# The last 256 output columns, one token tile at a time, with the layer norm of the first tile between the two

## The chip, the cores and the metric

The kernel runs on one core of a Trainium2 chip. The metric is the time of one execution in device microseconds; of a kernel that was run several times the median counts. The kernel before took 1534.78 us (median of three runs, 1531.65 to 1538.52).

The engines are named as in the profile: PE is TensorE (PEld its weight load), DVE is VectorE, ACT is ScalarE, POOL is GpSimd, and SP is the engine from whose queue nearly all transfers are issued here.

## What is computed

Two transformer-like blocks follow each other on 256 tokens of 2048 features, all in float32. The part that the change touches is the end of the second block: the last product (the output of the forgetting attention times `w_out`), the gated residual, and the layer norm that gives the result.

```python
def layer_norm(x, g, b):
    mu = jnp.mean(x, axis=-1, keepdims=True)
    var = jnp.mean(jnp.square(x - mu), axis=-1, keepdims=True)
    return (x - mu) * lax.rsqrt(var + EPS) * g + b

# last layer of the second block; y has 2048 features for each of the 256 tokens
out = y @ w_out
x = layer_norm(DN_ALPHA * x + gate[:, None] * out, ln_g[1], ln_b[1])
```

The mean and the variance of a token run over all 2048 columns, so nothing of a token's result can be written before its last column has been multiplied.

## The kernel before

**Tiling.** The 256 tokens are two token tiles of 128 (`ti` 0 and 1). Weights come in chunks of 128 x 1024 float32 (512 KB) from DRAM into one of seven `raw` buffers. ACT rounds a chunk to its high part `hi` (L1603), DVE forms the rest `lo` (L1605), and PE multiplies three times, high by high, high by low and low by high. `hi` and `lo` have three buffers each, and a chunk is prepared two chunks ahead of its use.

**The last product** (`o3` in the code). The first 1024 columns are one range of 16 chunks. The other 1024 columns are four ranges of 256 columns, each of four chunks, a chunk holding four row tiles of 256 columns. In `mm_tok` the activations are stationary and the weights stream: for each row tile, both token tiles get three products of 256 columns, so 24 products a chunk and 96 a range. Both token tiles of a range lie in one PSUM bank.

**After each range.** `evac_out(i)` runs on DVE: for the two token tiles the product times the gate (L1423), plus the residual (L1425), and the statistics of the finished columns (L1427, `bn_stats`). It is written in pairs: L1423 for both tiles, L1425 for both, L1427 for both. All 2048 columns of both tiles end up in `xk`, the first 1024 already times the gain.

**The bias rows.** After the third of the four ranges `evac_out` starts `bias_rows`, which puts the bias of the first 1024 columns under a product of one row of ones: four PE products of 1 x 128 by 1 x 512, two at the next step of the scheduler and two one chunk later. They fill four PSUM banks `vb`.

**The end.** `finish` runs after the last range, for both token tiles together. On DVE: the moments (L1452), the reciprocal root by `rsqrt` (L170 to L182, three rounds of two dependent steps, for one column a tile), with four operations of 512 columns (L1457, `center`) placed between the steps, and the row `wfo` = -mean times the root (L1461). Meanwhile `warm(20)` gives PE 20 products that nobody reads. Then PE turns `wfo` (L1466), ACT copies it (L1467), four one-row products add `wfo` times the gain into the `vb` banks, and DVE forms the eight pieces of 512 columns of the result (L1475), each followed by its store of 256 KB from the SP queue (L1476).

**What sets the order.** The program is written in one sequence by Python code: one loop over the chunks prepares, multiplies and calls the range's `evac`, and a small scheduler (`sched.tick`) advances side tasks once a chunk. Each engine runs its instructions in that order, and semaphores join the engines. Buffers of 128 x 1024 for the attention and the end come from one pool `blk` of 15.

Of the kernel before, what the change touches and what calls it, by code (L numbers as in the profile page):

```python
# [9 lines left out]
F32 = mybir.dt.float32  # L10
# [6 lines left out]
P = 128  # L17
# [15 lines left out]
W1 = 5  # L33
# [8 lines left out]
WARM = 20  # L42
# [30 lines left out]
class Slice:  # L73
    """Columns of a modulation product, summed over the 16 row tiles, per of them to a chunk; TensorE takes tiles pe."""
# [7 lines left out]
class Chunk:  # L82
    """Row tiles kts of a weight, 1024 / len(kts) columns of each."""
# [6 lines left out]
class Range:  # L90
    """Output columns of a product, 512 token columns to a bank; kind says which operand is stationary."""
# [7 lines left out]
def two_block_kernel(ctx: ExitStack, tc: tile.TileContext, a: dict, out: bass.AP):  # L99
# [47 lines left out]
    def warm(n):  # L147
        """Keeps TensorE's clock up while it waits: products that nothing reads."""
# [16 lines left out]
    def rsqrt(y, v, between=()):  # L165
        """rsqrt of two columns, in as few dependent steps as there can be; other work between the steps."""
        between = list(between)
        t, vh = t_([P, 2], "rq2"), t_([P, 2], "rqh")
# [4 lines left out]
        c = [slice(i, i + 1) for i in range(2)]  # L173
# [85 lines left out]
    def start(kind):  # L259
        """A head starts some ticks after the one before it."""  # L260
# [107 lines left out]
    def broadcast_cols(cols, dst):  # L368
        """cols: [128 tokens, n x 1]; dst [128, n*128] has each column along its free axis."""
# [12 lines left out]
    def dilated_tables():  # L382
        """-|t - s|, hugely negative where no dilation reaches s from t, and the number of dilations that do."""
# [28 lines left out]
    def retention_tables():  # L412
        """t - s where t >= s, s - t where s >= t, else huge, as [s, t]; the log decays."""
# [22 lines left out]
    def causal_tables():  # L436
        """s - t, hugely negative where s > t, blocks [(t1,s0) (t1,s1) (t0,s0)]; the mask of a diagonal block."""
# [17 lines left out]
    def logsig(dst, x, e, u, w):  # L455
        """min(x, 0) - log1p(exp(-|x|)), log1p(e) = 2 atanh(e / (2 + e))."""
# [59 lines left out]
    def colsum(sl):  # L516
        """Sums over partitions of the slice's columns, as columns [128, columns / 128]."""
# [22 lines left out]
    def shift_scale(sl, i, A, B, bshift, bscale, gain, beta, key):  # L540
        """A = gain * (1 + scale), B = shift + beta * (1 + scale) for the slice's column tiles from i on."""
# [41 lines left out]
    def mod_ss(w, ccol, A, B, bshift, bscale, gain, beta, key, i, n_=4):  # L583
        """Shift and scale of the features of n_ tiles from i on."""
# [37 lines left out]
    def affine_split(key, t, A, B, kt, fast=False):  # L622
        """First half of the split of A * t + B; returns the second half."""
# [62 lines left out]
    def begin_h(g):  # L686
        """Starts the activations that chunks up to g + HLEAD need; returns their second halves."""
# [11 lines left out]
    def mm_feat(r, ck, hi, lo):  # L699
        """Weights stationary: result [features, tokens]."""  # L700
# [9 lines left out]
    def mm_tok(r, ck, hi, lo):  # L710
        """Activations stationary: result [tokens, features]."""
# [27 lines left out]
    def add_range(w, c0, kts, kind, act, evac, per=1):  # L739
        """Columns c0.. of w over the row tiles kts, per row tiles to a chunk."""  # L740
# [7 lines left out]
    def add_segs(w, ranges, segs, act, evac):  # L748
        """segs: (indices of ranges, first row tile, last + 1), in order."""
# [5 lines left out]
    def gate_task(name):  # L755
        """z becomes 2 silu(z), in place."""
# [13 lines left out]
    # block 1 projections, in groups of row tiles  # L770
# [208 lines left out]
    def ret_gate(h):  # L979
# [4 lines left out]
        done("qkr", 2, 4)  # L984
        done("zr", 2, 4)

# [1 line left out]
    sums = {}  # L988

    def residual(r, k0, g):  # L990
# [702 lines left out]
```

## Time and profile before

| what | value |
|---|---|
| median of three runs | 1534.78 us (1531.65 to 1538.52) |
| profiled execution, span from the first to the last instruction | 1533.4 us |
| mean granted TensorE clock | 0.991 |
| PE busy | 1491.9 us, 97% of the span |
| DVE busy | 1264.8 us, 82% |
| ACT busy | 821.8 us, 54% |
| HBM read and written | 433.88 and 2.11 MB |
| last range of 256 columns, first to last product begun | 1499.55 to 1516.13 us |
| from the start of the last of them to the end of the last DVE operation | 1516.13 to 1530.20 us |

The span is the only time of that execution that the profile states, and it is the one against which the prediction's sum is made. Of its 1533.4 us, 3.2 us come after the last DVE operation: the last store and the end of the program. A line such as L145 is the line of the code that issued an instruction; L145 is the helper for every product. A product of float32 by float32 shows as two PE records, one of rounded parts as one.

### The profile page before, as it was taken

How to read it: one execution, taken by the hardware profiler on the slowest of the kernel's cores; microseconds unless marked ns; L12 is line 12 of the kernel's file. 1: busy time of each engine (PE TensorE's matmuls, PEld its weight loads, DVE VectorE, ACT ScalarE, POOL GpSimd, SP SyncE). 2: the span in 40 equal slices, each digit the busy share in tenths (PEclk: the TensorE clock that was granted, in tenths of full speed). 3: DMA queues.
4: the chain of work that ended last, by engine and by line, in shares of the span. 5: the costliest groups of instructions: out<-in, count | busy, mean ns of one | idle time of the engine just before them, and what ended most of it. 6: DMA issues, size and time to landing. Idle time of an engine off the chain costs nothing.

```text
span 1533.4 us, 26873 instructions
## 1 busy us (share of the span) xinstructions
PE 1491.9 (97%) x10190; PEld 1385.7 (90%) x10190; DVE 1264.8 (82%) x1832; ACT 821.8 (54%) x1532; POOL 49.6 (3%) x50
## 2 busy tenths in 40 slices
PE   5899999999999999999999999999999999999998
PEld 5889999989999798899998899978899999999897
DVE  5889989999988887987879988988887956667784
ACT  4474463655644657444555653465444776667530
POOL 3500000021000000000000000000000000000000
PEclk9999999999999999999999999999999999999998
DMA  9899979879699798999888889867899966878741
GB/s 321 289 353 338 344 273 324 309 255 328 213 322 326 250 366 282 343 343 311 254 297 286 295 301 320 272 210 250 320 354 324 338 231 199 260 259 292 259 152 56
DMA packets 180358, 437.77 MB, mean 285 GB/s; under 512 B 16352, under 2 KB 51314, under 8 KB 180228
## 3 DMA queue, kind: packets, MB, share of 16 engines
q1 hardware_dynamic: 179620, 435.89, 82.6%
q8 instruction: 80, 1.31, 0.3%
q14 instruction: 50, 0.41, 0.1%
q0 software_dynamic: 544, 0.14, 0.1%
q10 hardware_dynamic: 64, 0.02, 0.0%
HBM read 433.88 MB, written 2.11 MB: 284 GB/s over the span
## 4 chain that ended last, share of the span: by engine, by line
PE 81%; DVE 10%; ACT 3%; DMA 3%; issue 2%; SPq 0%; DVEq 0%; ACTq 0%
PE pa L145 74%; PE ps L145 4%; DVE lo L1605 4%; DVE acc L1588 3%; DMA w<-fdr 1%; ACT hi L1603 1%; PE ps L527 1%; DMA raw<-in_w_ada_dram 1%; DMA raw<-in_x_dram 1%; DVE hy L635 0%; DMA raw<-in_a_w_in_dram 0%; ACT w L632 0%; PE ps L1171 0%; DVE xT L656 0%; ACT blk L788 0%
## 5 line engine op out<-in xcount | busy, mean ns | idle before, releaser
L145 PE MATMUL pa<-hy,hi 128*128 128x256 f32 x4640 | 854.0, 286 | 8.7 <-ACT hy L631 2.7
L1603 ACT CAST hi<-raw 128x1024 fp32r<-128x1024 f32 x464 | 485.5, 1048 | 530.1 <-PE pa L145 444.2
L145 PEld LDWEIGHTS pa<-hy,hi 128*128 128x128 f32 x4640 | 726.3, 192 | 14.1 <-ACT hy L631 3.1
L1605 DVE TENSOR_TENSOR lo<-raw,hi 128x1024 fp32r<-128x1024 f32 x464 | 568.9, 1228 | 204.5 <-ACT hi L1603 200.8
L145 PE MATMUL pa<-hy,lo 128*128 128x256 f32 x2320 | 658.9, 284 | 1.9 <-DVE lo L1605 1.9
L145 PE MATMUL pa<-hi,hy 128*128 128x512 f32 (+1 forms) x1536 | 463.7, 380 | 3.2 <-ACT hy L631 2.3
L145 PEld LDWEIGHTS pa<-hy,lo 128*128 128x128 f32 x2320 | 445.5, 192 | 2.9 <-DVE lo L1605 2.5
L1588 DVE SCALAR_TENSOR_TENSOR acc<-raw,cact,acc 128x1024 f32<-128x1024 f32 (+2 forms) x343 | 423.0, 1236 | 8.8 <-DMA raw<-in_w_ada_dram 8.0
L145 PEld LDWEIGHTS pa<-hi,hy 128*128 128x128 f32 x1536 | 284.4, 192 | 58.7 <-ACT hy L631 3.4
L145 PE MATMUL pa<-lo,hy 128*128 128x512 f32 (+1 forms) x768 | 288.5, 376 | 1.1 <-DVE lo L1605 1.1
L145 PEld LDWEIGHTS pa<-lo,hy 128*128 128x128 f32 x768 | 147.2, 192 | 26.1 <-DVE lo L1605 1.7
L788 ACT ACTIVATE blk<-pa 128x512 f32<-128x512 f32 (+1 forms) x96 | 51.7, 578 | 10.9 <-PE pa L145 8.3
L535 ACT ACTIVATE jk<-ps 128x128 f32<-128x128 f32 x158 | 43.6, 276 | 9.9 <-PE ps L527 6.1
L792 DVE TENSOR_TENSOR blk<-pa,blk 128x512 f32<-128x512 f32 x60 | 37.4, 681 | 0.3 <-PE pa L145 0.3
L145 PE MATMUL ps<-blk,blk 128*128 128x256 f32 (+1 forms) x176 | 37.3, 342 | 0.0
L145 PEld LDWEIGHTS ps<-blk,blk 128*128 128x128 f32 x176 | 30.1, 190 | 3.3 <-DVE blk L792 0.2
L635 DVE TENSOR_TENSOR hy<-w,hy 128x256 fp32r<-128x256 f32 x64 | 27.1, 425 | 5.9 <-ACT w L632 4.9
L535 ACT ACTIVATION_READ_ACCUMULATOR jk<-ps 128x1 f32 x158 | 30.7, 195 | 0.0
L1573 POOL MEMSET acc<- 128x1024 f32 x2 | 1.9, 950 | 859.7 <-PE ps L527 859.7
L632 ACT ACTIVATE w<-xT,B,A 128x256 f32<-128x256 f32 x32 | 19.2, 600 | 11.3 <-DVE xT L662 11.3
L527 PE MATMUL ps<-ident,acc 128*128 128x128 f32 x160 | 24.6, 278 | 0.0
L634 ACT CAST hy<-w 128x256 fp32r<-128x256 f32 x58 | 23.6, 407 | 1.9
(295 smaller groups left out, 821.1 us busy)
## 6 DMA issues: line engine op xcount, KB each, us to landing
raw<-in_w_mod_dram SPq DMA_DIRECT2D x192, 512.0 KB, 5.3
raw<-in_a_w_in_dram SPq DMA_DIRECT2D x128, 512.0 KB, 5.6
raw<-in_w_in_dram SPq DMA_DIRECT2D x112, 512.0 KB, 5.4
raw<-in_w_ada_dram SPq DMA_DIRECT2D x80, 512.0 KB, 5.4
raw<-in_kv_w_mod_dram SPq DMA_DIRECT2D x64, 512.0 KB, 6.0
raw<-in_kv_w_dram SPq DMA_DIRECT2D x64, 512.0 KB, 5.3
raw<-in_b_w_in_dram SPq DMA_DIRECT2D x64, 512.0 KB, 5.0
raw<-in_w_out_dram SPq DMA_DIRECT2D x32, 512.0 KB, 5.3
```

The costliest lines, as they stand in the source:

```text
L145: PE.matmul(o, l, r, start=start, stop=stop, skip_group_check=True)
L527: PE.transpose(pt[:, j * P : (j + 1) * P], sl.acc[:, (q + j) * P : (q + j + 1) * P], ident)
L535: AC.activation(jk, pt[:, j * P : (j + 1) * P], AF.Copy, accum_out=r[:, q + j : q + j + 1])
L632: AC.activation(hf, t, AF.Identity, bias=bi, scale=sc)
L634: AC.copy(h[:, 0, :], hf)
L635: V.tensor_tensor(h[:, 1, :], hf, h[:, 0, :].bitcast(F32), op=ALU.subtract)
L788: AC.activation(dst, src, AF.Copy, scale=sc)
L792: V.tensor_tensor(dst, src, dst, op=ALU.add)
L1573: GP.memset(sl.acc, 0.0)
L1588: V.scalar_tensor_tensor(ac, tn, c, ac, op0=ALU.mult, op1=ALU.add)
L1603: AC.copy(hi, t)
L1605: V.tensor_tensor(lo, t, hi.bitcast(F32), op=ALU.subtract)
```

## The change

The first three ranges of 256 columns stay, but `evac_out` now finishes one token tile (`add_part`: times the gate, plus the residual, statistics) before it turns to the other.

The last range has a kind of its own, `last`, and two PSUM banks, one for each token tile. Its chunks are multiplied for tile 0 as they come, and kept; the `hi` and `lo` of its fourth chunk take two `blk` buffers, since the three `hi` and `lo` buffers hold the first three chunks. Then tile 0 goes through its statistics, its root and its first two stores, while PE multiplies the same four chunks for tile 1. After three of these four chunks PE turns tile 0's row, and after the fourth it makes tile 0's products. `finish` then treats tile 1 alone, with tile 0's other two pieces and stores in between.

The bias rows are gone. `wfo` has a second column of ones, and the gain and the bias lie in two rows of one buffer, so that one product of two rows gives the shift and the bias together: four such products instead of four for the bias and four for the shift. Twenty unread products become five. The bias of the last 1024 columns is loaded earlier in the SP queue. Docstrings and comments are removed.

```diff
-WARM = 20
+WARM = 5
...
-        for nm in "gb":
-            yield need_blk(1)
-            lnr[nm + "r", 0] = blk()
-            nc.sync.dma_start(lnr[nm + "r", 0][0:1, :], a[f"ln_{nm}_2"][1:2, 0:CW])
+        yield need_blk(1)
+        lnr["gb"] = blk()
+        for i, nm in enumerate("gb"):
+            nc.sync.dma_start(lnr["gb"][i : i + 1, :], a[f"ln_{nm}_2"][1:2, 0:CW])
         yield need_blk(1)
         lnr["b"] = blk()
         nc.sync.dma_start(lnr["b"], a["ln_b_2"][1, CW:D].partition_broadcast(P))
...
+    def add_part(i, ti, src):
+        x = out_part(ti, CW + i * S, S)
+        t = t_([P, S], "w1", W1)
+        V.tensor_tensor(t, src, gbc[1][:, i * S : (i + 1) * S], op=ALU.mult)
+        V.tensor_tensor(x, x, t, op=ALU.add)
+        V.bn_stats(bst[:, ti, 2 + i, :], x)
...
-            for ti in (1, 0):
-                V.tensor_tensor(t[ti], r.banks[0][:, ti * S : (ti + 1) * S], gbc[1][:, i * S : (i + 1) * S], op=ALU.mult)
-            for ti in range(2):
-                V.tensor_tensor(x[ti], x[ti], t[ti], op=ALU.add)
-            for ti in range(2):
-                V.bn_stats(bst[:, ti, 2 + i, :], x[ti])
-            if i == 2:
-                sched.add(bias_rows(), front=True)
-            if i == 3:
-                finish()
+            for ti in (1, 0):
+                add_part(i, ti, r.banks[0][:, ti * S : (ti + 1) * S])
...
+    def shifts(wr):
+        u = []
+        for c in range(2):
+            u.append(pacc.tile([P, 512], F32, tag="acc", name=uid("pa")))
+            mm(u[c], wr[0:2, 0:P], lnr["gb"][0:2, c * 512 : (c + 1) * 512], True, True)
+        return u
...
+    def mm_last(r, ck, hi, lo):
+        r.kept.append((ck, hi, lo))
+        one_tile(r, 0, [r.kept[-1]])
+        if not ck.last:
+            return
...
+        add_part(3, 0, r.banks[0][:, 0:S])
+        moments(0, [lambda c=c: center(0, c) for c in (2, 3)])
+        for c in (2, 3):
+            store(0, c, lnb(c))
+        one_tile(r, 1, r.kept[:3])
+        wr = shift_row(0)
+        one_tile(r, 1, r.kept[3:])
+        r.u0 = shifts(wr)
...
+    def finish(r):
+        add_part(3, 1, r.banks[1][:, 0:S])
+        moments(1, [lambda: center(1, 2), lambda: store(0, 0, r.u0[0]), lambda: center(1, 3),
+                    lambda: store(0, 1, r.u0[1])])
         warm(WARM)
+        u = shifts(shift_row(1))
         for c in (2, 3, 0, 1):
+            store(1, c, u[c] if c < 2 else lnb(c))
...
+            if ck.kind == "last" and ck.last:
...
+                hi, lo = (blkp.tile([P, CW], F32R, tag="blk", name=uid("blk")) for _ in range(2))
```

Three places in the order of the instructions follow. The first is DVE between the third and the fourth range, before. `w` is the product times the gate, `blk_15291` and `blk_15380` are tiles 0 and 1 of the last 1024 columns, and the last two rows prepare the third and fourth chunk of the last range.

```order
L1423 TENSOR_TENSOR w_16598<-pa_16488,blk_16209 128x256
L1423 TENSOR_TENSOR w_16597<-pa_16488,blk_16209 128x256
L1425 TENSOR_TENSOR blk_15291<-blk_15291,w_16597 128x256
L1425 TENSOR_TENSOR blk_15380<-blk_15380,w_16598 128x256
L1427 BN_STATS bst<-blk_15291 128x6
L1427 BN_STATS bst<-blk_15380 128x6
L1605 TENSOR_TENSOR lo_16610<-raw_16392,hi_16609 128x1024
L1605 TENSOR_TENSOR lo_16643<-raw_16422,hi_16642 128x1024
```

The same place after the change, where `blk_15299` and `blk_15388` are tiles 0 and 1:

```order
L1419 TENSOR_TENSOR w_16604<-pa_16495,blk_16216 128x256
L1420 TENSOR_TENSOR blk_15388<-blk_15388,w_16604 128x256
L1421 BN_STATS bst<-blk_15388 128x6
L1419 TENSOR_TENSOR w_16608<-pa_16495,blk_16216 128x256
L1420 TENSOR_TENSOR blk_15299<-blk_15299,w_16608 128x256
L1421 BN_STATS bst<-blk_15299 128x6
L1645 TENSOR_TENSOR lo_16613<-raw_16399,hi_16612 128x1024
L1645 TENSOR_TENSOR blk_16631<-raw_16429,blk_16630 128x1024
```

The pairs have become two chains of three dependent operations, and the two `lo` operations still stand behind them.

The second place is PE from the end of the third range into the fourth, before; `ps_16605` and `ps_16607` are banks of the bias, `pa_16613` is the bank of the last range.

```order
L145 MATMUL pa_16488<-lo_16514,hy_15986 128x256
L145 MATMUL pa_16488<-hi_16513,hy_15986 128x256
L145 MATMUL ps_16605<-blk_15825,ones 128x512
L145 MATMUL ps_16607<-blk_15825,ones 128x512
L145 MATMUL pa_16613<-hi_16541,hy_15259 128x256
L145 MATMUL pa_16613<-lo_16542,hy_15259 128x256
```

After the change nothing stands between the ranges; the row of tile 0 is turned inside the products of tile 1 (`pa_16617`), between its third and its fourth chunk (`blk_16630` and `blk_16631` are that chunk's high and low part):

```order
L145 MATMUL pa_16617<-hi_16612,hy_15933 128x256
L145 MATMUL pa_16617<-lo_16613,hy_15933 128x256
L145 MATMUL pa_16617<-hi_16612,hy_15933 128x256
L1451 MATMUL ps_16732<-ident,wfo_125 2x128
L145 MATMUL pa_16617<-blk_16630,hy_15935 128x256
L145 MATMUL pa_16617<-blk_16631,hy_15935 128x256
```

The four bias products have left PE's queue, and one turning product that waits for DVE now stands ahead of tile 1's last twelve products.

The third place is the end of PE's queue, before; `xT` with `ident` are the unread products.

```order
L145 MATMUL pa_16755<-xT,ident 128x256 x20
L1466 MATMUL ps_16776<-ident,wfo 1x128 x2
L145 MATMUL ps_16605<-blk_15823,s_16777 128x512
L145 MATMUL pa_16638<-blk_15823,s_16777 128x512
L145 MATMUL ps_16607<-blk_15823,s_16777 128x512
L145 MATMUL pa_16640<-blk_15823,s_16777 128x512
```

And after:

```order
L145 MATMUL pa_16748<-blk_15831,s_16734 128x512
L145 MATMUL pa_16750<-blk_15831,s_16734 128x512
L145 MATMUL pa_16776<-xT,ident 128x256 x5
L1451 MATMUL ps_16782<-ident,wfo_126 2x128
L145 MATMUL pa_16786<-blk_15831,s_16784 128x512
L145 MATMUL pa_16788<-blk_15831,s_16784 128x512
```

Tile 0's two products have moved ahead of the unread ones, and two instead of four follow the last turning.

## Rows read from the trace of the kernel before

**Rows 1.** The chain that ended last, from 1440 us: start, length, engine and line.

```profile
1497.71 1.91 PE ps L145 x4
```

**Rows 2.** Stretches: length; busy us of PE, PEld, DVE, ACT, POOL; granted clock; DMA.

```profile
1461.00:1497.43 36.43, 36.43 (x294) 35.39 (x293) 28.92 (x41) 13.54 (x14) 0.00 (x0) 1.00 0.42 134
1497.43:1499.55 2.12, 2.12 (x7) 0.74 (x5) 1.77 (x5) 1.04 (x1) 0.00 (x0) 1.00 0.04 8
1499.55:1503.90 4.35, 4.35 (x24) 4.35 (x24) 1.54 (x3) 0.00 (x0) 0.00 (x0) 0.61 0.00 0
1503.90:1506.02 2.12, 2.12 (x8) 0.74 (x6) 0.73 (x1) 1.04 (x1) 0.00 (x0) 1.00 0.00 0
1506.02:1516.25 10.23, 10.23 (x74) 10.23 (x74) 0.50 (x1) 0.00 (x0) 0.00 (x0) 0.83 0.00 0
```

**Rows 3.** PE in order of time, around the end of the third range: start, length, operation.

```profile
1496.59 0.28 PE L145 MATMUL pa<-lo,hy 128*128 128x256 f32 x1
...
1496.95 0.28 PE L145 MATMUL pa<-lo,hy 128*128 128x256 f32 x1
...
1500.94 0.41 PE L145 MATMUL pa<-lo,hy 128*128 128x256 f32 x1
...
1501.58 0.41 PE L145 MATMUL pa<-lo,hy 128*128 128x256 f32 x1
```

**Rows 4.** PE in order of time, from the last product of the last range.

```profile
1516.13 0.28 PE L145 MATMUL pa<-hi,hy 128*128 128x256 f32 x1
1516.25 8.79 PE L145 MATMUL pa<-xT,ident 128*128 128x256 f32 x40
1524.88 0.38 PE L1466 MATMUL ps<-ident,wfo 128*1 128x128 f32 x2
1525.71 1.12 PE L145 MATMUL ps<-blk,s 1*128 1x512 f32 x2 [0.45 <-ACT s L1467]
```

**Rows 5.** DVE in order of time, third range's end and after the last product.

```profile
1499.88 1.21 DVE L1605 TENSOR_TENSOR lo<-raw,hi 128x1024 fp32r<-128x1024 f32 x1
...
1516.45 0.75 DVE L1423 TENSOR_TENSOR w<-pa,blk 128x256 f32<-128x256 f32 x2 [9.93 <-PE pa L145]
1517.23 0.76 DVE L1425 TENSOR_TENSOR blk<-blk,w 128x256 f32<-128x256 f32 x2
...
1518.58 0.47 DVE L1452 BATCH_NORM_AGGREGATE mvo<-bst 128x2 f32<-128x36 f32 x2
1519.08 0.17 DVE L1453 TENSOR_SCALAR vfo<-mvo 128x2 f32<-128x2 f32 x1
...
1519.57 0.74 DVE L1457 SCALAR_TENSOR_TENSOR blk<-blk,mvo,blk 128x512 f32<-128x512 f32 x1
1520.23 0.34 DVE L178 SCALAR_TENSOR_TENSOR rq<-yfo,rqh 128x1 f32<-128x1 f32 x2
...
1523.64 0.16 DVE L1461 SCALAR_TENSOR_TENSOR wfo<-mvo,yfo 128x2 f32<-128x2 f32 x1
...
1526.87 0.75 DVE L1475 SCALAR_TENSOR_TENSOR blk<-blk,yfo,ps 128x512 f32<-128x512 f32 x1 [0.42 <-PE ps L145]
...
1529.45 0.75 DVE L1475 SCALAR_TENSOR_TENSOR blk<-blk,yfo,pa 128x512 f32<-128x512 f32 x1
```

**Rows 6.** DVE operations after 1516.3 us by line: count, busy us, mean ns, idle.

```profile
L178 DVE SCALAR_TENSOR_TENSOR rq<-yfo,rqh 128x1 f32<-128x1 f32 x6 | 1.0, 214 | 0.0
L1423 DVE TENSOR_TENSOR w<-pa,blk 128x256 f32<-128x256 f32 x2 | 0.8, 420 | 9.9 <-PE pa L145 9.9
```

**Rows 7.** Two earlier stretches in which PE stood idle; columns as in rows 2.

```profile
1355.40:1361.20 5.80, 3.38 (x27) 3.33 (x28) 1.58 (x2) 5.66 (x11) 0.00 (x0) 1.00 0.74 268
999.50:1007.80 8.30, 4.61 (x12) 2.88 (x13) 5.45 (x27) 4.72 (x10) 0.00 (x0) 0.83 0.15 58
```

**Rows 8.** The SP queue in order of time: start, length, line, transfer.

```profile
1414.77 0.23 SPq L1378 DMA_DIRECT2D blk<-in_ln_b_dram  x1
1419.04 2.65 SPq L1552 DMA_DIRECT2D raw<-in_b_w_out_dram  x2
...
1430.57 0.37 SPq L1381 DMA_DIRECT2D blk<-in_ln_b_dram  x1
```

More of the change, by code (lines that the diff above doesn't have):

```diff
@@ L172, in rsqrt @@
         V.tensor_scalar(yi, yi, -1, 0x5F3759DF, op0=ALU.mult, op1=ALU.add)
-        c = [slice(i, i + 1) for i in range(2)]
+        c = [slice(i, i + 1) for i in range(n_)]
         for _ in range(3):
@@ L1384, in two_block_kernel @@
     bst = c_([P, 2, 6, 6], "bst")
-    vb = {}
     def out_part(ti, c0, n_):
@@ new lines, in f, with center @@
+                add_part(i, ti, r.banks[0][:, ti * S : (ti + 1) * S])
+        return f
+    mvo = [c_([P, 2], f"mvo{ti}") for ti in range(2)]
+    vfo = [c_([P, 1], f"vfo{ti}") for ti in range(2)]
+    yfo = [c_([P, 1], f"yfo{ti}") for ti in range(2)]
+    wfo = [c_([P, 2], f"wfo{ti}") for ti in range(2)]
+    def center(ti, c):
+        x = out_part(ti, c * 512, 512)
+        V.scalar_tensor_tensor(x, x, mvo[ti][:, 0:1], lnr["g", 1][:, (c - 2) * 512 : (c - 1) * 512],
+                               op0=ALU.subtract, op1=ALU.mult)
@@ new lines, in moments, with shift_row @@
+    def moments(ti, between):
+        V.bn_aggr(mvo[ti], bst[:, ti, :, :].rearrange("p a b -> p (a b)"))
+        V.tensor_scalar(vfo[ti], mvo[ti][:, 1:2], 1e-5, None, op0=ALU.add)
+        rsqrt(yfo[ti], vfo[ti], between)
+        V.scalar_tensor_tensor(wfo[ti][:, 0:1], mvo[ti][:, 0:1], -1.0, yfo[ti], op0=ALU.mult, op1=ALU.mult)
+    def shift_row(ti):
+        pw = ptile()
+        PE.transpose(pw[0:2, 0:P], wfo[ti], ident)
+        wr = t_([P, 512], "s", 4)
+        AC.copy(wr[0:2, 0:P], pw[0:2, 0:P])
+        return wr
@@ new lines, in shifts, with store, lnb @@
+    def shifts(wr):
[4 more added lines that the diff above has]
+        return u
+    def store(ti, c, u):
+        x = out_part(ti, c * 512, 512)
+        V.scalar_tensor_tensor(x, x, yfo[ti], u, op0=ALU.mult, op1=ALU.add)
+        nc.sync.dma_start(out[0, ti * P : (ti + 1) * P, c * 512 : (c + 1) * 512], x)
+    def lnb(c):
+        return lnr["b"][:, (c - 2) * 512 : (c - 1) * 512]
@@ new lines, in mm_last @@
+    def mm_last(r, ck, hi, lo):
[3 more added lines that the diff above has]
+            return
+        sched.until(lambda: ("g3", 1) in ready and ("xk", 1) in ready and "lnb" in ready)
+        for ti in range(2):
+            V.tensor_scalar(wfo[ti][:, 1:2], ones[:, 0:1], 1.0, None, op0=ALU.mult)
+        add_part(3, 0, r.banks[0][:, 0:S])
[6 more added lines that the diff above has]
+        r.u0 = shifts(wr)
@@ L1480, in two_block_kernel @@
     add_range(wo3, 0, list(range(KT)), "tok", "y3", evac_out0)
-    for i in range(4):
+    for i in range(3):
         add_range(wo3, CW + i * S, list(range(KT)), "tok", "y3", evac_out(i), 4)
+    add_range(wo3, CW + 3 * S, list(range(KT)), "last", "y3", finish, 4)
+    gi[-1].rng.nb, gi[-1].rng.kept = 2, []
     gpos["end"] = len(gi)
```

59 lines of the change are left out of this document (18 added, 41 removed).

## The prediction

> **What bounds the kernel now.** I read three views in this order: the chain that ended last, the busy times by stretch, and PE and DVE in order of time over the last 40 us. From 1461 us until the end of the third range PE is busy for 36.43 of 36.43 us at a granted clock of 1.00 [rows 2], so PE sets the time there and nothing that DVE, ACT or the queues do ends it. A product of 256 columns is worth 0.12 us there: three of them fit between 1496.59 and 1496.95 [rows 3]. The last range, 96 such products, should take 11.5 us. It starts where the third ends, at 1497.43, and its last product starts at 1516.13 [rows 4], 18.7 us later. Where the rest went is the first thing to see: the four one-row bias products stand on the chain [rows 1], and twice 2.12 us pass from the product ahead of a pair of them to the product behind it [rows 2]. [...]
>
> After the last product the bound changes hands. DVE runs a chain for both token tiles, from 1516.45 to the row `wfo` at 1523.80 [rows 5]. PE's unread products run on until the turning starts at 1524.88 [rows 4], so they hold it back. From there four products and DVE's four pieces follow, the last ending at 1530.20 [rows 5]. The span ends 3.2 us later.
>
> **The change, part by part.** The sum is made against the profiled execution, span 1533.4 us. The median is 1534.78, 1.4 above; I take the gain from the profile and subtract it from the median.
>
> *Bias products removed.* Two pairs, each 2.12 us less the 0.12 that a step costs anyway [rows 2]: 2.0 each, 4.0 us on PE, all of it on the path, since PE is what everything waits for.
>
> *Slow products after them.* 23 steps take 4.35 us instead of 2.76, and the 72 steps from 1506.02 take 10.23 instead of 8.64 [rows 2]: 1.6 us each, 3.2 us. With the bias products gone, the cause is gone. Whether every execution of the kernel before has both slow stretches no row tells, so 0 to 3.2 is the bound; I take 3.2, as measured. Without further waits the last product would start at 1516.13 - 4.0 - 3.2 = 1508.95.
>
> *A wait that comes in: the third chunk of the last range.* For tile 0 alone a chunk is twelve products, 1.44 us, so the last range eats its chunks twice as fast. The third chunk's `hi` can only be cast when the third range has released the buffer, and its `lo` stands on DVE behind the range's six operations, now in two chains. One such operation is 0.42 us [rows 6], a dependent one starts 0.03 after it (1516.45 + 0.75 to 1517.23) and an independent one 0.08 before its end: 2.5 us for six, against 2.13 in pairs (1516.45 to 1518.58) [rows 5]. DVE starts at 1497.75, 0.32 after the product at 1497.43, so `lo` starts at 1500.25 and ends 1.21 later [rows 5], at 1501.46. PE wants it at 1500.55: a wait of 0.95 us. The fourth chunk's `lo` ends near 1502.6, when PE is still in the third. Bounds: 0, if PE is behind anyway, to 1.2, the length of one `lo`.
>
> [...]
>
> *A second wait: the turning of tile 0's row.* It stands in PE's queue behind 36 products of tile 1, 4.32 us, and twelve products are queued behind it. Tile 0's last product starts at 1497.55 + 47 x 0.12 + 0.95 = 1504.13 and DVE starts at 1504.45. Its chain: three dependent operations 1.35, the moments and the first root steps 1.0 less one 0.22 aggregation, that is 0.78 (1518.58 to 1519.57) [rows 5], two `center` steps at 0.66 with a one-column step of 0.13 between them (1519.57 to 1520.23, and half of the 0.34 for two, less overlap) [rows 5], then five one-column steps that wait for each other, 0.19 to 0.25 each from the mean of 214 ns [rows 6], and `wfo` 0.16: 4.8 us. PE arrives at 1508.57 and goes on at 1509.29: 0.7 us, and the turning itself takes some 0.3 of PE. Together 1.0 us; bounds 0.3 and 2.0, a 20% longer chain. Who waits for it: tile 1's last twelve products and so the whole end. Tile 0's two first pieces and stores run on DVE and SP while PE multiplies; they cost nothing as long as tile 1's products (1509.6 to 1511) cover DVE's 1.4 us. So the last product starts at 1508.95 + 0.95 + 1.0 = 1510.9, 5.2 us earlier than before.
>
> *The end.* Before, 1516.13 to 1530.20 is 14.1 us. After, for tile 1 alone: 0.32 until DVE starts; the chain until `wfo` 2.13 as for tile 0 (1.35 + 0.78), then two `center` steps and two pieces of tile 0 at 0.66, in place of the four `center` steps of before, and single one-column steps: 5.9 us against 7.35. The turning starts 0.25 after `wfo`, not 1.08, since five unread products end long before: 0.8 less. One turning instead of two: 0.1 less. Two products instead of four: DVE's first dependent piece starts 1.16 after the product starts [rows 4, 5], the second 0.86 later, a third of 1526.87 to 1529.45, and ends 0.75 after that [rows 5]; the other two, 1.72 us, are gone. In sum 14.1 - 1.5 - 0.8 - 0.1 - 1.7 = 10.0, a gain of 4.1.
>
> What speaks against the whole 4.1 is the clock. Ahead of tile 1's last two products PE has two-row products for 1.7 us, five unread products for 2.2 and then some 2 us of nothing; before, twenty unread ones filled that place. At half the clock those two products would take 1.8 us more. The nearest rows point both ways: 2.4 us without any product left the clock at 1.00 over 1355.40 to 1361.20, three waits close together brought it to 0.83 over 999.50 to 1007.80 [rows 7], and one-row products brought it down each time. I take half of the 1.8 for a median of executions, and keep 0 and 1.8 for the range.
>
> *At nothing.* The broadcast of the bias is issued some 15 us earlier in the SP queue; PE is busy throughout, and the queue had nothing to issue until 1419.04 [rows 8]. In the first two ranges the chains add 0.4 us to DVE, which idles longer than that in each chunk; were it not so, PE would wait by that 0.4.
>
> *Sum.* 4.0 + 3.2 - 0.95 - 1.0 + 4.1 - 0.9 = 8.4 us. 1534.78 - 8.4 = **1526.4 us**. With the last products at full clock it is 9.3, 1525.5.
>
> **The rivals.** *Slow clock in the new end* (0.12): both new waits and the unread gap let the clock fall; one slow stretch among the products as measured, 1.6, and the full 1.8 at the end: gain 9.3 - 3.4 = 5.9, 1528.9. Rows 7 give one case for it and one against. [...]
>
> *The slow stretches were not the rule* (0.15): executions of the kernel before mostly have one of the two or none, so part of the 3.2 us isn't there to be won. Gain 8.4 - 1.6 = 6.8 to 5.2, about 1528.5. For it: the clock did not always fall after a weak stretch [rows 7]. Against: both pairs were followed by one.
>
> *Waits that don't come* (0.12): the two waits shrink to 0.6 and 0.3 and the end keeps its clock: gain 10.3, 1524.5.
>
> *Slower than before* (0.05): the 512 KB broadcast now stands in the SP queue where a 4 KB row stood, and takes that row's buffer. If the buffer were not free, every weight behind it would be held. Nothing is held until 1419.04, when the next weight is issued; were it free only at 1430.57, when the broadcast went out before [rows 8], the weights would be 11.5 us late, and the time 3.1 us more than before, 1537.9. It decides from a release at 1427.4 on. Against it: the row in the same place of the pool went out at 1414.77 without a wait.
>
> **How the numbers follow.** Forecast 0.55, the rivals 0.12, 0.15, 0.12 and 0.05, and 0.01 for none of these. More than 0.5% is 7.7 us, about what a measurement of this kernel can tell from no change. The forecast lies just beyond it; with runs that spread by 3 to 4 us around their median I give it 0.38 faster and 0.17 the same. The missing waits add 0.12 and the slow stretches 0.03 to faster, the rest of these and the slow clock 0.24 to same. So 0.53, 0.42, 0.05. The range: the low end is the best case, 1524.5, less 2 us for the spread; the high end is no slow stretches and the full 1.8 at the end, 4.0 - 1.95 + 2.3 = 4.4, 1530.4, and a little for the spread: 1522.5 to 1531.
>
> **What would show it.** In the profile after: no one-row products, and 0.12 us a step with a clock of 1.00 through the third and fourth range; a gap near 1 us on PE ahead of the third chunk's `lo`, and one near 0.7 ahead of the turning; the last range of both tiles in 13.5 us instead of 18.7; some 10 us from the last product to DVE's end; the last two two-row products in 0.43 us a record, or 0.86 if the clock fell. Wrong would be: a clock under 0.9 in the last range, waits of PE for `lo` beyond 1.2 us, or PE waiting for weights after 1415 us.

## The result, and the profile after

The changed kernel took 1528.87 us (median of 11 runs, 1526.38 to 1534.87) beside 1538.02 us for the kernel before (median of 11, the first three runs among them): a ratio of 0.9948, 95% interval 0.9931 to 0.9964, or 8.0 us less than 1534.78 (5.5 to 10.6). The ratio is formed from the fast runs alone, without one run of the kernel before that took 3744.63 us, and is not the quotient of the two medians. A second set, 7 runs, gave 1526.91 us and again 0.9948 (0.9928 to 0.9969). The forecast was 8.4 us less, 1526.4 us, in a range of 1522.5 to 1531.0.

The profiled execution has a span of 1527.3 us, 6.1 us below the 1533.4 of the kernel before. The busy times by stretch around the change, in the columns of [rows 2] (PE, PEld, DVE, ACT and POOL busy with the number of instructions, then the granted clock and what the transfers moved):

```profile
1461.00:1499.04 38.04, 38.04 (x301) 36.57 (x299) 30.55 (x41) 13.75 (x15) 0.00 (x0) 1.00 0.44 139
1499.04:1502.04 3.00, 3.00 (x28) 3.00 (x26) 2.54 (x7) 2.00 (x2) 0.00 (x0) 1.00 0.02 5
1506.00:1510.46 4.46, 4.46 (x38) 4.25 (x36) 4.00 (x15) 0.00 (x0) 0.00 (x0) 1.00 0.00 0
1518.94:1524.20 5.26, 4.04 (x5) 1.23 (x5) 2.76 (x4) 0.25 (x1) 0.00 (x0) 0.56 0.53 199
1357.57:1363.00 5.43, 5.43 (x31) 5.25 (x32) 3.12 (x4) 5.43 (x11) 0.00 (x0) 0.69 0.50 158
```

The clocks of 0.61 and 0.83 in [rows 2] are gone; the last range runs at 1.00. A new half-speed stretch is at the very end (0.56). The last row lies far ahead of the change: in the kernel before, a stretch of the same work kept 1.00 [rows 7]. There the profiled execution fell behind: its third range ends at 1499.04, 1.6 us later than before (1497.43) [rows 2], with the same products ahead of it.

PE in order of time (start, us, engine, line, operation, count, and in brackets the idle time ahead of it and who ended it), from the wait for the third chunk to the last products:

```profile
1503.13 0.38 PE L145 MATMUL pa<-lo,hy 128*128 128x256 f32 x1 [0.81 <-DVE lo L1645]
...
1511.20 0.27 PE L1451 MATMUL ps<-ident,wfo 128*2 128x128 f32 x1 [0.74 <-DVE wfo L1446]
1511.23 1.68 PE L145 MATMUL pa<-blk,hy 128*128 128x256 f32 x12
1512.83 1.98 PE L145 MATMUL pa<-blk,s 2*128 2x512 f32 x4
1514.74 2.43 PE L145 MATMUL pa<-xT,ident 128*128 128x256 f32 x10
1518.94 0.27 PE L1451 MATMUL ps<-ident,wfo 128*2 128x128 f32 x1 [1.77 <-DVE wfo L1446]
1519.55 3.77 PE L145 MATMUL pa<-blk,s 2*128 2x512 f32 x4 [0.34 <-ACT s L1453]
```

Both waits that the prediction named are there, 0.81 us ahead of the third chunk's `lo` and 0.74 us ahead of the turning. The two-row products (four records) take 1.98 us for tile 0 and 3.77 us for tile 1: the same instructions at full and at half speed (granted clock 1.00 over 1512.83 to 1514.74 and 0.50 over 1519.55 to 1523.32).

DVE in the same stretch, the rows that open and close its chains:

```profile
1499.36 0.42 DVE L1419 TENSOR_TENSOR w<-pa,blk 128x256 f32<-128x256 f32 x1 [0.57 <-PE pa L145]
...
1501.52 0.43 DVE L1421 BATCH_NORM_STATS2 bst<-blk 128x6 f32<-128x256 f32 x1
1501.87 1.21 DVE L1645 TENSOR_TENSOR lo<-raw,hi 128x1024 fp32r<-128x1024 f32 x1
...
1506.18 0.43 DVE L1419 TENSOR_TENSOR w<-pa,blk 128x256 f32<-128x256 f32 x1 [1.84 <-PE pa L145]
...
1510.89 0.16 DVE L1446 SCALAR_TENSOR_TENSOR wfo<-mvo,yfo 128x1 f32<-128x1 f32 x1
1510.97 1.41 DVE L1466 SCALAR_TENSOR_TENSOR blk<-blk,yfo,blk 128x512 f32<-128x512 f32 x2
1512.94 0.42 DVE L1419 TENSOR_TENSOR w<-pa,blk 128x256 f32<-128x256 f32 x1 [0.56 <-PE pa L145]
...
1518.72 0.16 DVE L1446 SCALAR_TENSOR_TENSOR wfo<-mvo,yfo 128x1 f32<-128x1 f32 x1
...
1523.36 0.75 DVE L1466 SCALAR_TENSOR_TENSOR blk<-blk,yfo,pa 128x512 f32<-128x512 f32 x1 [0.96 <-PE pa L145]
```

These rows give a measure that leaves out whatever happened before the changed part. DVE begins an evacuation 0.3 us after the start of a range's last product (except in B of e5 and e6, where DVE itself comes late), so four of its times cut the end of any of these kernels into three stretches: **A**, from the evacuation of the third range to the next one (tile 0's, or both tiles' where they stay together); **B**, from tile 0's to tile 1's; **C**, from the last evacuation to the end of DVE. For before, 1497.75 to 1516.45 to 1530.20 [rows 5]: 18.70 and 13.75. For after, 1499.36, 1506.18, 1512.94 and 1523.36 + 0.75 = 1524.11: 6.82, 6.76 and 11.17.

| profile | A | B | C | A+B+C | half speed in it |
|---|---|---|---|---|---|
| before | 18.70 | - | 13.75 | 32.45 | two stretches in A |
| before, again | 18.69 | - | 15.66 | 34.35 | two in A, last products |
| after | 6.82 | 6.76 | 11.17 | 24.75 | last products |
| after, again | 6.83 | 6.75 | 9.38 | 22.96 | unread products |
| e1: one product for both rows | 11.52 | - | 15.61 | 27.13 | last products |
| e2: one-row products back | 9.95 | 6.76 | 9.46 | 26.17 | unread products |
| e2, again | 9.95 | 6.75 | 9.46 | 26.16 | unread products |
| e8: the same with 128 rows | 9.18 | 6.76 | 10.60 | 26.54 | last products |
| e3: low parts first | 5.75 | 6.76 | 10.14 | 22.65 | last products |
| e4: nine unread products | 6.83 | 6.76 | 10.86 | 24.45 | unread products |
| e5: turning late | 6.82 | 6.13 | 9.46 | 22.41 | unread products |
| e6: e3 and e5 | 5.76 | 6.12 | 10.38 | 22.26 | last products |
| e11: shift with 128 rows | 6.83 | 6.80 | 9.45 | 23.08 | none |
| e12: e3, e5, e11, one piece later | 5.76 | 5.76 | 10.29 | 21.81 | last products |

### The profile page after: what moved, and what is told of

Read it like the earlier page. It is cut to its first block, busy times and chain, and to the rows that moved or that the text cites. A ratio compares the mean times of both kernels' runs of the same rounds, so it can differ in the third digit from the quotient of the medians.

```text
span 1527.3 us, 26803 instructions
## 1 busy us (share of the span) xinstructions
PE 1482.3 (97%) x10152; PEld 1376.9 (90%) x10152; DVE 1267.4 (83%) x1839; ACT 821.7 (54%) x1533; POOL 49.5 (3%) x50
## 4 chain that ended last, share of the span: by engine, by line
PE 77%; DVE 12%; DMA 5%; ACT 3%; issue 2%; SPq 0%; DVEq 0%; ACTq 0%
PE pa L145 71%; DVE lo L1645 4%; PE ps L145 4%; DVE acc L1623 3%; DMA w<-fdr 2%; DMA raw<-in_w_ada_dram 2%; ACT hi L1643 2%; PE ps L528 1%; DMA raw<-in_w_in_dram 1%; DMA raw<-in_a_w_in_dram 0%; DVE hy L636 0%; ACT blk L789 0%; ACT w L633 0%; PE ps L1172 0%; DVE xT L657 0%
## 5 line engine op out<-in xcount | busy, mean ns | idle before, releaser
L145 PE MATMUL pa<-hi,hy 128*128 128x512 f32 (+1 forms) x1520 | 457.3, 379 | 3.1 <-ACT hy L632 2.3
L145 PEld LDWEIGHTS pa<-hi,hy 128*128 128x128 f32 x1520 | 279.0, 189 | 56.7 <-ACT hy L632 3.1
L145 PE MATMUL pa<-lo,hy 128*128 128x512 f32 (+1 forms) x760 | 284.9, 375 | 2.2 <-DVE lo L1645 2.2
```

The costliest lines, as they stand in the source:

```text
L145: PE.matmul(o, l, r, start=start, stop=stop, skip_group_check=True)
```

## The experiments

**The kernel before and the changed one, once more.** No edit; is what the first profiles showed the rule?

> The kernel before once more, for one profile. My prediction took 3.2 us from two slow stretches behind the bias products, which one execution showed. If they are the rule, this execution has both again: 23 steps in some 4.35 us behind the first pair and a last stretch of some 10.2 us behind the second. If they are a matter of chance in each execution, one or both take 0.12 us a step (2.76 and 8.64 us) at a clock of 1.00.

> The changed kernel once more, beside the three above. My theory gives a ratio to before of 0.995 as in its first runs, and again a clock of about 0.56 under its last two products, since what stands ahead of them is fixed; if the clock's fall there is a matter of chance in each execution, the four records take 1.7 us here instead of 3.77 and the end is 1.8 us earlier.

Before, again, by stretch: the two stretches behind the bias products, and from the turning to the end; then PE's unread products:

```profile
1496.30:1500.80 4.50, 4.50 (x25) 4.43 (x24) 1.54 (x3) 0.00 (x0) 0.00 (x0) 0.62 0.00 0
1502.78:1512.85 10.07, 10.07 (x72) 10.07 (x72) 0.50 (x1) 0.00 (x0) 0.00 (x0) 0.83 0.00 0
1521.62:1528.85 7.23, 5.99 (x11) 1.93 (x9) 4.57 (x7) 0.36 (x1) 0.00 (x0) 0.67 0.66 254
```

```profile
1512.99 8.79 PE L145 MATMUL pa<-xT,ident 128*128 128x256 f32 x40
```

Both slow stretches are back in the same places, and A is 18.69 again. In addition the last products fell to half speed here (0.67, C 1.9 us longer), which the first profile of before did not show, although the same twenty unread products stand ahead of them. After, again, PE at its end:

```profile
1517.89 1.98 PE L145 MATMUL pa<-blk,s 2*128 2x512 f32 x4
1519.80 4.11 PE L145 MATMUL pa<-xT,ident 128*128 128x256 f32 x10
1524.00 0.27 PE L1451 MATMUL ps<-ident,wfo 128*2 128x128 f32 x1
1524.61 1.98 PE L145 MATMUL pa<-blk,s 2*128 2x512 f32 x4 [0.34 <-ACT s L1453]
```

The clock fell here too, but under the five unread products (4.11 us, against 2.43 in the first profile). They filled the time in which PE waits for `wfo` anyway, and the last products ran at full speed. That is worth 1.8 us of C, 9.38 against 11.17. I had expected a fall in the same place each time; the ratio to before, 0.9948, was as expected.

**e1: the rows in one product.** With it come the loads that this needs, and two small DVE operations after the third range that write the column of ones; the order of the token tiles stays.

```diff
             if i == 2:
-                sched.add(bias_rows(), front=True)
+                sched.until(lambda: "lnb" in ready)
+                for ti in range(2):
+                    V.tensor_scalar(w[:, ti, 1:2], ones[:, 0:1], 1.0, None, op0=ALU.mult)
...
-                mm(vb[ti, c], wr[0:1, ti * P : (ti + 1) * P], lnr["gr", 0][0:1, c * 512 : (c + 1) * 512], False, True)
+                vb[ti, c] = pacc.tile([P, 512], F32, tag="acc", name=uid("pa"))
+                mm(vb[ti, c], wr[0:2, ti * P : (ti + 1) * P], lnr["gb"][0:2, c * 512 : (c + 1) * 512], True, True)
```

> The kernel before with one edit: the bias rows are gone, and gain and bias lie in two rows of one buffer, so that the four products after the last range give shift and bias together. Both token tiles stay together, the evacuation stays in pairs, the unread products stay at twenty. My theory (the bias products cost their own 4.0 us and about 3.2 us of half-speed products after them, and this is the larger part of the change's gain): about 7.2 us less than before, ratio near 0.9953; in the profile the last range takes 11.5 us from its first to its last product at a clock of 1.00, and the 14.1 us behind its last product are unchanged. Rival (the slow stretches are not the rule in executions of before): 4.0 to 5.6 us less, ratio 0.9964 to 0.9974. Second rival (the merged rows are worth little, the token-by-token order brought the gain): under 3 us less.

Measured: 1530.0 us beside 1535.44, ratio 0.9964 (0.9951 to 0.9977), 5.5 us less. The last range, and the stretch from its first shift product to the end:

```profile
1498.63:1510.15 11.52, 11.52 (x98) 11.52 (x97) 4.65 (x10) 2.09 (x2) 0.00 (x0) 1.00 0.00 1
1519.74:1526.08 6.34, 5.55 (x8) 1.84 (x8) 3.73 (x6) 0.00 (x0) 0.00 (x0) 0.63 0.69 267
```

A is 11.52 us, 96 steps of 0.12: all 7.2 us came out of the last range. 1.9 us of them went again at the end, which took 6.34 us at a clock of 0.63 where the first profile of before took 4.49 (1525.71 to 1530.20). So 32.45 - 27.13 = 5.3 us are left beside the first profile of before, and 34.35 - 27.13 = 7.2 beside the second, whose end was slow too. The median, 5.5 us, is what the rival gave, but its interval (3.5 to 7.5) also holds the 7.2 of my theory, so the times do not decide between them. The rival's reason is in neither profile of before: both have both slow stretches.

**e2: four one-row products put back into the changed kernel**, unread, at the old places (one chunk apart, which is twelve products here and was 24 before):

```diff
+            if i == 2:
+                sched.add(one_row(), front=True)
...
+    def one_row():
+        for _ in range(2):
+            for c in range(2):
+                pd = ptile()
+                mm(pd, ones[0:1, :], lnr["gb"][0:1, c * 512 : (c + 1) * 512], True, True)
+            yield
```

> The changed kernel with four one-row products of 512 columns put back that nothing reads, two behind the third range and two one chunk later, where the bias products stood before. My theory: they cost 4.0 us of their own and up to 3.2 us of slow products, less the 0.95 us wait for the third chunk's low part, which PE then no longer meets because it is 2 us late already: 4.6 to 6.3 us more than the changed kernel, so 1 to 4 us less than before. The granted clock falls below 0.7 in the 4 us behind a pair. Rival (the products cost only their own time): 3.0 to 4.0 us more than the changed kernel at a clock of 1.00.

> The kernel with the one-row products put back, once more for a profile: its first profile has no slow stretch and lies 6 us below the median of its runs. My theory (the clock's fall behind one-row products is what separates its fast executions from the others): an execution near the median of 1534.3 us shows one or two slow stretches of some 15 products behind the one-row products, 1.6 us each, and half-speed products in the end; one near 1528.5 shows none.

**e8: the same with all 128 rows**, `mm(pd, ident, lnr["g", 1][:, ...], True, True)` in place of the one-row product:

> The changed kernel with four unread products of 512 columns put back at the two places behind the third range, as in the kernel with the one-row products put back, but with all 128 rows in use. Own time the same: in the profile of that kernel, which has no slow stretch, the way from the third range's evacuation to tile 0's is 9.95 us against 6.82 in the changed kernel, 3.1 us more; its median is 7.4 us more. My theory (it is the single row that brings the clock down, not the interruption of the accumulation): 3.1 us more than the changed kernel in the median too, no product of 256 columns behind them at half speed. Rival (any such products between the others bring it down): 5 to 7.4 us more.

Measured: e2 1534.31 us beside 1535.44, ratio 0.9985 (0.9970 to 1.0000), some 5.7 us more than the changed kernel by the ratios; e8 1530.84 beside 1535.36, ratio 0.9970 (0.9956 to 0.9984), some 3.4 us more. By stretch from the first pair to the second and from there to tile 0's evacuation, e2 and then e2 again; then e8, from the first pair to tile 0's evacuation; then PE's rows of e2's first pair and of e8's two:

```profile
1497.11:1500.65 3.54, 3.54 (x18) 2.15 (x17) 3.29 (x7) 1.99 (x2) 0.00 (x0) 1.00 0.00 0
1500.65:1507.17 6.52, 6.52 (x43) 5.27 (x43) 1.55 (x4) 0.00 (x0) 0.00 (x0) 1.00 0.00 0
```

```profile
1502.27:1505.80 3.53, 3.53 (x17) 2.15 (x16) 3.29 (x7) 1.99 (x2) 0.00 (x0) 1.00 0.00 0
1505.80:1512.33 6.53, 6.53 (x43) 5.28 (x43) 1.55 (x5) 0.00 (x0) 0.00 (x0) 1.00 0.00 0
```

```profile
1505.62:1515.00 9.38, 9.38 (x60) 7.46 (x59) 4.84 (x10) 2.00 (x2) 0.00 (x0) 1.00 0.01 2
```

```profile
1497.11 1.98 PE L145 MATMUL ps<-blk,ones 1*128 1x512 f32 x4
```

```profile
1505.62 1.88 PE L145 MATMUL ps<-blk,ident 128*128 128x512 f32 x4
...
1508.77 1.88 PE L145 MATMUL ps<-blk,ident 128*128 128x512 f32 x4
```

The clock is 1.00 in all these stretches. Here my theory fell: four pairs of one-row products, in two executions 5 us apart, were followed by no slow product. The second execution, 1533.56 us, lies near the median of e2; that it was 5 us slower than the first has its cause ahead of the changed part, for its third range's evacuation begins 5.2 us later. What a pair costs of its own can be read: from one pair to the next, twelve products away, 3.54 us with one row and 3.15 with 128 rows (1505.62 to 1508.77), which is 12 x 0.12 for the twelve and 4 x 0.43 for the pair. The one-row pair takes 0.39 us more. Against the changed kernel, whose 1.07 us wait they hide, the four products lengthen A by 3.1 and 2.4 us. For e8 that is within 1 us of what its ratio says; of e2's 5.7 us some 2.6 are in neither profile, and with intervals of 2 to 3 us on both sides that may be scatter.

**e3: the low parts first.** Tile 1's half of the third range's evacuation stands behind the low parts of the third and fourth chunk on DVE:

```diff
+                if i == 2 and ti == 1:
+                    late.append(r.banks[0])
...
+        if len(r.kept) == 1:
+            add_part(2, 1, late[0][:, S : 2 * S])
         r.kept.append((ck, hi, lo))
```

> The changed kernel, with tile 1's half of the third range's evacuation moved behind the low parts of the third and fourth chunk of the last range on DVE; nothing else moves. In the two profiles of the changed kernel PE stands idle for 0.81 us ahead of the third chunk's low part, because DVE has the six operations of the evacuation in front of it. My theory: that low part starts right behind its cast, 1.2 us earlier, the idle 0.81 us is gone, and the stretch from the last product of the third range to the end of DVE is 0.9 us shorter, the fourth chunk without a wait of its own; tile 0's chain starts 0.9 us earlier and the 0.74 us wait ahead of the turning stays. Rival (the cast of the third chunk's high part, held until the third range gives its buffer back, is the true limit): the idle time shrinks by 0.3 us or less.

**e5: the turning late**, behind tile 1's last product:

```diff
-        wr = shift_row(0)
         one_tile(r, 1, r.kept[3:])
-        r.u0 = shifts(wr)
+        r.u0 = shifts(shift_row(0))
```

> The changed kernel, with the turning of tile 0's row moved behind tile 1's last product, where in the changed kernel it stands ahead of tile 1's last twelve products. My theory: the 0.74 us in which PE waits for wfo and the 0.27 of the turning come off the path, tile 1's last product starts 1.0 us earlier, and PE's new wait for ACT's copy (0.3 to 0.6 us) lies beside DVE's chain for tile 1 and costs nothing: 1.0 us less than the changed kernel. Rival (the shift products now come later than DVE wants them for tile 0's first piece inside tile 1's chain): that piece waits, wfo of tile 1 comes up to 1 us later, and nothing is gained. Clock: where the last products run at half speed the end is 1.8 us longer, as in the changed kernel.

**e6: both, with four unread products.**

> Both edits together (tile 1's half of the evacuation behind the low parts, the turning of tile 0's row behind tile 1's last product), and four unread products in place of five, since nine of them, run at half speed, held the turning of tile 1's row back by 1.5 us. My theory: the two waits and one turning, 1.9 us, come off the path; 1.9 us less than the changed kernel, ratio to before near 0.9935. PE then has no idle time from the third range to tile 1's last product. Rival (with the waits gone the clock falls elsewhere, or DVE becomes the bound): under 1 us less.

Measured: e3 1527.99 us beside 1536.4, ratio 0.9944 (0.9925 to 0.9964); e5 1525.11, 0.9928 (0.9905 to 0.9952); e6 1526.99, 0.9933 (0.9910 to 0.9957). The intervals all hold the 0.9948 of the changed kernel, so the medians do not tell these versions apart from it; the stretches do. DVE of e3:

```profile
1500.34 0.43 DVE L1419 TENSOR_TENSOR w<-pa,blk 128x256 f32<-128x256 f32 x1 [0.58 <-PE pa L145]
...
1501.60 1.21 DVE L1652 TENSOR_TENSOR lo<-raw,hi 128x1024 fp32r<-128x1024 f32 x1
...
1506.09 0.42 DVE L1419 TENSOR_TENSOR w<-pa,blk 128x256 f32<-128x256 f32 x1 [0.79 <-PE pa L145]
```

`lo` starts 1.26 us after the evacuation instead of 2.51, and A is 5.75, the 48 products and nothing else. The wait was worth 1.07 us, and the operations ahead of `lo` on DVE were its cause; the cast was not. In e5, B fell from 6.76 to 6.13 only, not to 5.76. Its DVE shows why:

```profile
1509.23 0.16 DVE L1446 SCALAR_TENSOR_TENSOR wfo<-mvo,yfo 128x1 f32<-128x1 f32 x1
1509.31 1.41 DVE L1466 SCALAR_TENSOR_TENSOR blk<-blk,yfo,blk 128x512 f32<-128x512 f32 x2
1510.64 0.41 DVE L1419 TENSOR_TENSOR w<-pa,blk 128x256 f32<-128x256 f32 x1
```

There is no bracket on the last row: DVE goes from tile 0's two pieces straight to tile 1's evacuation, without waiting for PE. With PE's wait gone, DVE's work for tile 0 had become the bound, 0.37 us behind PE. e6 has both gains and the same bound: A is 5.76 and B 6.12.

**e4: nine unread products in place of five**, `WARM = 9`.

> The changed kernel with nine unread products in place of five between tile 0's and tile 1's shift products. In its profile the five end 1.77 us before wfo releases the turning, and the last two products (four records) take 3.77 us at a granted clock of 0.56, where the same records of the kernel before take 0.43 each. My theory (the idle stretch brings the clock down): nine products end within 0.2 us of wfo, the four records take 1.7 us, and the kernel takes 1.8 us less than the changed one where that one lost it, 0.9 in the median of several if it loses it every other time. Rival (two-row products bring the clock down whatever stands between, as one-row products did): the last records still take 0.86 us each, no change.

Measured: 1527.66 us beside 1535.44, ratio 0.9951 (0.9932 to 0.9969), no change beside the 0.9948 of the changed kernel. PE at its end, and DVE's `wfo`:

```profile
1512.47 1.98 PE L145 MATMUL pa<-blk,s 2*128 2x512 f32 x4
1514.38 5.84 PE L145 MATMUL pa<-xT,ident 128*128 128x256 f32 x18
1520.06 0.27 PE L1451 MATMUL ps<-ident,wfo 128*2 128x128 f32 x1
1520.67 1.98 PE L145 MATMUL pa<-blk,s 2*128 2x512 f32 x4 [0.34 <-ACT s L1453]
```

```profile
1518.36 0.16 DVE L1446 SCALAR_TENSOR_TENSOR wfo<-mvo,yfo 128x1 f32<-128x1 f32 x1
```

The last products are at full speed, but the unread ones fell to half speed and took 5.84 us, not the 3.9 of 18 records at 0.22. `wfo` was ready at 1518.52 (1518.36 + 0.16), and the turning started at 1520.06: what had been meant to keep the clock up was late by 1.5 us.

**e11: the shift products with all 128 rows.** Row 0 is the shift, row 1 the ones, the others zero against rows of the gain:

```diff
-    wfo = [c_([P, 2], f"wfo{ti}") for ti in range(2)]
+    wfo = [c_([P, P], f"wfo{ti}") for ti in range(2)]
...
-            mm(u[c], wr[0:2, 0:P], lnr["gb"][0:2, c * 512 : (c + 1) * 512], True, True)
+            mm(u[c], wr[:, 0:P], lnr["g", 0][:, c * 512 : (c + 1) * 512], True, True)
```

> The changed kernel with its four two-row shift products made with all 128 rows: row 0 the shift, row 1 the ones, the other 126 rows zero against rows of the gain; the two turnings are of 128 columns in place of 2, and the row of the bias goes into the gain's buffer by the POOL queue. Same columns, so the same own time at full speed. In five of the profiles so far some of the products behind a turning ran at half speed: the last two of the kernel, or the unread ones ahead of them. My theory (few rows bring the clock down): the last four records take 0.43 us each and the ten unread ones 2.2 us in all, 1.50 to 1.58 us from wfo to tile 1's first dependent piece, and the median is 0.9 to 1.8 us below the changed kernel's. Rival (zero rows or the waits for wfo bring it down all the same): half-speed records as before, no change.

**e12: e3, e5 and e11 together**, and tile 0's piece of the last 512 columns behind tile 1's:

```diff
-        for c in (2, 3, 0, 1):
-            store(1, c, u[c] if c < 2 else lnb(c))
+        for ti, c in ((1, 2), (1, 3), (0, 3), (1, 0), (1, 1)):
+            store(ti, c, u[c] if c < 2 else lnb(c))
```

> Four edits to the changed kernel: tile 1's half of the third range's evacuation behind the low parts, the turning of tile 0's row behind tile 1's last product, the shift products with all 128 rows, and, new here, tile 0's piece of the last 512 columns moved on DVE from the front of tile 1's evacuation to behind tile 1's own two pieces, where DVE waits for the shift products anyway. With the first two edits DVE's evacuation of tile 1 begins 6.12 us after that of tile 0, though 48 products are 5.76: DVE had become the bound by 0.36. My theory: 5.76 to 5.8 us between the two evacuations, the last four records 0.43 us each, and 20.5 us from the third range's evacuation to DVE's end, against 24.75 and 22.96 in the two profiles of the changed kernel and 22.26 with the first two edits; 2.5 to 4.2 us less than the changed kernel, ratio to before 0.992 to 0.993. Rival (half speed comes back at the end): 22.2 us on that way, and 1.5 us less than the changed kernel.

Measured: e11 1529.89 us beside 1535.36, ratio 0.9955 (0.9939 to 0.9971); e12 1527.27 beside 1534.71, ratio 0.9951 (0.9932 to 0.9969). The last products of e11 and, in the second fence, of e12:

```profile
1515.73 1.88 PE L145 MATMUL pa<-blk,s 128*128 128x512 f32 x4
1517.45 2.32 PE L145 MATMUL pa<-xT,ident 128*128 128x256 f32 x10
1521.93 0.33 PE L1450 MATMUL ps<-ident,wfo 128*128 128x128 f32 x1 [2.15 <-DVE wfo L1445]
1522.61 1.98 PE L145 MATMUL pa<-blk,s 128*128 128x512 f32 x4 [0.35 <-ACT s L1452]
```

```profile
1509.12 2.32 PE L145 MATMUL pa<-xT,ident 128*128 128x256 f32 x10
1512.87 0.33 PE L1455 MATMUL ps<-ident,wfo 128*128 128x128 f32 x1 [1.42 <-DVE wfo L1450]
1513.55 2.83 PE L145 MATMUL pa<-blk,s 128*128 128x512 f32 x4 [0.36 <-ACT s L1457]
```

e11 shows no slow record, in spite of 2.15 us without a product; e12, with a shorter wait (1.42), shows 2.83 us for the last four, the last two of them at half speed (DVE's two pieces behind them begin at 1514.72 and 1516.42, 1.70 us apart, against 0.86 in the first profile of before). So the number of rows does not decide it alone. In e12, A and B are 5.76 us each: both waits and DVE's 0.36 are out, and 21.81 us is the shortest end of all. I had expected 20.5, or 22.2 with half speed at the end, and half speed it was. In the medians nothing of it can be seen: e12 was to be 2.5 to 4.2 us below the changed kernel and e11 0.9 to 1.8, and none of these versions is measured as better than the changed kernel.

## Why the prediction was right

The total was 8.4 us against 8.0 measured. The measured interval, 5.5 to 10.6, also holds the gains of three rivals (5.9, 6.8 and 10.3), so the total alone does not single out the forecast; the stretches have to. I had put 0.53 on a gain of more than 0.5%: it is 0.52%, with an interval of 0.36 to 0.69, so that stays undecided. By its steps:

- **Bias products, 4.0, and slow products behind them, 3.2.** Right, as terms: A of before is 18.7 in both profiles, and 11.52 with that edit (e1); expected were 11.5. The cause that I gave for the slow products, the single row, is not shown: in e2 the clock stayed at 1.00 behind four pairs. What the runs do show is that they were there in both executions of before and in none of the 12 profiles without the bias rows. Against the rival (slow stretches not the rule) stand these two profiles out of two; the times of e1 leave room for it.
- **The wait for the third chunk, 0.95.** The prediction's own figures give 1501.46 - 1500.55 = 0.91, 0.04 less than it wrote; measured is 1.07. PE lost 0.97 (the next product was due at 1502.16 and started at 1503.13) and 0.1 on starting again (0.22 to the product behind it, at 1503.35, in place of 0.12). Its mechanism held to the row: predicted 2.5 us from the evacuation to `lo`, measured 2.51; e3 took it away by order alone. In the trace an operation that needs the one ahead started 0.04 us after its end (1499.82 after 1499.36 + 0.42), and `lo`, which doesn't, started 0.08 before it (1501.87, the one ahead until 1501.95); the same six operations in pairs let `lo` start after 2.13 us (1497.75 to 1499.88, before), in a chain after 2.51. The rival of the waits that don't come (gain 10.3) puts 0.6 on this wait, which no run shows: with tile 1's half of the evacuation ahead of `lo` it was 1.07, and with that half behind it there was none (e3).
- **The turning, 1.0.** B is 6.76, exactly 1.0 above 48 products. What I did not see: DVE's own work for tile 0 was only 0.63 us behind that wait, so taking the wait away gives 0.63 and not 1.0 (e5), until a piece is moved too (e12).
- **The end, 4.1.** C is 9.38 where no product on the path is slow, against 13.75: 4.4. The 0.3 more is in part the turning, which starts 0.06 us after `wfo` (1518.94 after 1518.88) and not 0.25. The chain from tile 1's evacuation to the end of `wfo` took 5.94 us (1512.94 to 1518.88) against the predicted 5.9.
- **Half clock at the last products, half of 1.8.** The size was right: 11.17 against 9.38, at a granted clock of 0.50 under them. Of six profiles with this same end (after twice, e2 twice, e3, e8) the last products were slow in three, by 1.8, 0.8 and 1.2 us against 9.38, on average 0.65 over the six. What I had left out is that the kernel before can lose it too: 15.66 against 13.75, 1.9 us, in its second profile. The rival (slow clock in the new end) is what the first profile after shows, without the slow stretch among the products that was part of it.
- **At nothing.** PE is busy for 95.00 of 95.00 us from 1400 to 1495 us, and for 38.04 of 38.04 up to the end of the third range, so neither the broadcast nor the chains of the first ranges held it. The slower rival fell.

In the two first profiles the sum can be closed: A+B+C fell by 32.45 - 24.75 = 7.7 us (predicted for a slow end: 9.3 - 1.8 = 7.5), and the stretch ahead of it was 1.6 us later, which leaves the 6.1 us between the spans. With both profiles of each kernel the mean end is 33.40 and 23.86, 9.5 us apart, within the measured interval and nearer to the 9.3 that I had before I took off 0.9 for the clock. The kernel before pays that loss as well, in one of two profiles, so taking it off the change alone was an error; that the measured 8.0 came so near to 8.4 is in part luck.

**What stays open.** What makes the clock fall at one place and not at another; e2, e11 and e12 rule out the row count as the whole answer. And how much of the further 0.6 to 2.1 us that e3, e5, e6 and e12 take out of A and B would show in the time: the third range's evacuation begins between 1494.50 and 1505.82 us in the 14 profiles, a scatter of 11 us that hides it; two executions of one and the same kernel already differ there by 3.25 us (before) and 5.06 us (after).

## What to carry to other kernels

One-row products put between large ones on the engine that sets the time cost more here than the same columns with 128 rows, 0.39 us a pair; a row more in a product that is made anyway did the same work for nothing, for four records take 1.98 us with one row (e2) and with two (after). When a wait is taken off one engine, look at once at which engine is next and by how little. Unread products that are meant to keep the clock up should fit their gap at half speed too, or they hold back what they were meant to help (e4); no run here shows that they do keep it up.

## What the runs showed of the hardware

- Each of the nine profiles with two-row shift products and unread products behind tile 1's last product (after and e2 twice, e3, e4, e5, e6, e8) has one half-speed stretch there: under the unread products (five profiles; 3.74 to 4.11 us for the ten records against 2.43 in the first profile of after, 5.84 for the 18 of e4) or under the last ones (four; 2.75 to 3.77 us for the four records against 1.98). What it cost went by the place: nothing where PE waits anyway (C 9.38 to 9.46), 0.8 to 1.8 us on the path, and 1.5 us in e4, where the slow unread products reached into the path.
- A pair of one-row products, four records, held PE 0.39 us longer than the same pair with 128 rows, 3.54 against 3.15 us from pair to pair.
- The clock fell while PE was never idle: in the profile of before PE is busy for 4.35 of 4.35 us at a granted clock of 0.61 and for all of the 2.12 us ahead of them, which hold a pair of one-row products [rows 2]; in e11 it stayed up after 2.15 us without a product.
